# Wider passes in the tail of a streaming encoder step: merges go through DRAM scratch and run beside the last attention blocks, outputs follow tile by tile

## The chip, the cores and the metric

One core of a Trainium2 chip runs the whole program. The metric is the device time of one execution in microseconds (us), median of several runs. The engines are PE (TensorE, matmuls; PEld is its weight load), DVE (VectorE), ACT (ScalarE), POOL (GpSimd) and SP (SyncE, which here issues every DMA). SBUF is the on-chip memory, PSUM the accumulators that PE writes.

## What is computed

One layer of a mixer over 2048 prompt tokens, 16 meta tokens and 8 x 16 sample tokens, width 1024. From the normalised rows h one input projection feeds two branches: gated linear attention (its output, per token, is called `oa` here) and sparse attention over selected keys (`ob`, already gated). Then, per token:

```
y_a    = oa @ w_gla
y_b    = ob @ w_dsa
merged = sigmoid(m_a + gate_b[0]) * y_a + sigmoid(m_b + gate_b[1]) * y_b
h_new  = layer_norm(ALPHA * h + merged @ w_out, ln_g, ln_b)
```

All matrices are 1024 x 1024. The meta tokens need no output, so the tail handles 17 tiles of 128 tokens: prompt tiles 0 to 15 and the sample tile "s". In scratch they stand in the order 0, 1, 2, ..., 15, s.

## The kernel before

Each fp32 product is made of three matmuls: every operand is split into a rounded part `hi` and a remainder `lo` (cast on ACT, subtraction on DVE or POOL), and `mm3` (L265 to L267) adds hi*hi, hi*lo and lo*hi over eight slices of 128 rows, 24 matmuls in all. The weight side of a matmul is 128 x 128, the moving side has as many columns as the piece of tokens is wide.

Phase 1 projects the input and selects keys. Phase 2 runs attention in blocks of 128 queries, 15 down to 8 with the linear attention beside them, and then the tail, which is what the change touches: the blocks of `LAST` (7, 6, 5, 0, 4, 2, 1, 3), and beside and after them three products.

- `gla_project` (L1374) multiplies w_gla with `oa`, 242 tokens a pass in 9 passes (`PASSA`), eight steps of 128 output channels each (24 matmuls, into the one PSUM bank of `pd`), multiplies with the gate `ma` on DVE (`rma`) and stores to the DRAM scratch `d_ya`. It is a generator; `LAST` says how many passes are emitted after each block.
- `merge` (L1392) does the same with w_dsa and `ob`, adds `ya`, and splits the sum into `mh`/`ml`, which stay in SBUF (two pairs of 256 tokens). A step of it is: load `ya` (`rya`) and `mb` (`rmb`), 24 matmuls, multiply and add on DVE, cast on ACT, subtract on POOL.
- `finish` (L1405) merges in chunks of 256 tokens (eight) and one of 128. The first two merges are emitted while attention's pools are still open; then w_out is loaded and split (`woh`, `wol`), and outputs (`fo`, 48 matmuls of 512 columns per 128 tokens, then residual and layer norm) alternate with the next merges.

`w3` (L1339) loads and splits weights. w_gla and w_dsa use the same SBUF tiles `wh`/`wl`, one after the other: each of its eight sets can be reloaded when the last pass of the gated projection has read it. `x3` (L1355) loads and splits four pieces of activations, `rows3` (L1362) loads one 128-row slice into one of two buffers. SP issues the DMAs in the order in which the program has them, and an SP instruction that waits holds up those behind it. The order of all instructions on their engines is laid down at build time by a planner that simulates the program; a block is only given a priority by its place in the code (`early` and `later` shift it). What the lines of a profile call by helper lines: L144 is `tt` (elementwise with two tensors), L153 `stt`, L156 `act`, L159 `copy`, L1347 the cast in `w3`.

## Time and profile before

| | us |
|---|---|
| median of three runs | 3597.57 |
| lowest, highest | 3590.15, 3598.61 |
| profiled execution | 3593.96 |
| its span, first to last instruction | 3592.2 |
| PE busy in it | 3483.6 |
| DVE, ACT, POOL busy | 2528.4, 1450.9, 1088.8 |

The span is what the trace covers; the profiled execution is 1.8 us longer than it. A group of instructions is named by its line, engine, operation and by what it writes and reads (`out<-in`); the shapes are partitions x elements. A matmul's duration in the trace is longer than the distance to the next one, since they overlap. [...]

### The profile page before, as it was taken

Reading aid. Unit: us, or ns where it says so; the run is one execution under the profiler, and the core shown is the slowest. Engines: PE = TensorE matmul, PEld = TensorE weight load, DVE = VectorE, ACT = ScalarE, POOL = GpSimd, SP = SyncE. Lnnn points to the kernel's source line nnn. Section 1 sums busy time; section 2 is a strip of 40 time slices with the busy share of each in tenths; the row PEclk is TensorE's granted clock in tenths of the full one; section 3 lists DMA queues with packets and bytes.
Section 4 is the critical chain, followed back from the end, with each engine's and each line's share of the span. In section 5 each row is a group of like instructions: output and inputs, shape, how many; then the busy total and the mean of one; then the engine's idle time right before and its main releaser. Section 6 shows DMA issues by size and latency. Waiting matters only on the chain. (4 is left out here: it accounts for less than half of the span.)

```text
span 3592.2 us, 66024 instructions
## 1 busy us (share of the span) xinstructions
PE 3483.6 (97%) x24196; PEld 3212.5 (89%) x24196; DVE 2528.4 (70%) x5813; ACT 1450.9 (40%) x3092; POOL 1088.8 (30%) x1412
## 2 busy tenths in 40 slices
PE   7999999999999998999999999999999999989999
PEld 6999999999999998998887788888877888879998
DVE  7737998799999998964436677676765666544444
ACT  4435223433324323322535556566565344331110
POOL 3122242242342334434411345455410000022221
PEclk9999999999999999999999999999999999999999
DMA  8642443254442345445573433333343345564431
GB/s 265 202 131 82 139 121 108 83 157 127 119 145 73 103 134 148 140 134 159 171 199 94 122 109 97 102 105 99 100 121 88 89 120 135 151 192 136 124 115 62
DMA packets 550340, 457.77 MB, mean 127 GB/s; under 512 B 95248, under 2 KB 522528, under 8 KB 550016
## 3 DMA queue, kind: packets, MB, share of 16 engines
q1 hardware_dynamic: 550016, 453.56, 43.9%
q8 instruction: 190, 3.11, 0.4%
q14 instruction: 134, 1.10, 0.1%
HBM read 292.49 MB, written 160.92 MB: 126 GB/s over the span
## 5 line engine op out<-in xcount | busy, mean ns | idle before, releaser
L144 POOL TENSOR_TENSOR wlo<-raw,whi 128x512 fp32r<-128x512 f32 x360 | 482.3, 1360 | 817.1 <-ACT whi L159 706.7
L150 DVE TENSOR_SCALAR_CACHE_REDUCE junk<-sc,cand 128x272 bf16<-128x272 f32 (+6 forms) x512 | 701.6, 1370 | 16.9
L265 PE MATMUL pp<-whi,xh 128*128 128x256 f32 (+3 forms) x1952 | 562.1, 288 | 3.5 <-ACT whi L159 2.3
L265 PE MATMUL pp<-xh,whi 128*128 128x384 f32 (+2 forms) x1728 | 563.6, 326 | 1.9 <-ACT whi L159 1.1
L267 PE MATMUL pp<-whi,xl 128*128 128x256 f32 (+3 forms) x1952 | 560.8, 288 | 4.4 <-DVE xl L144 4.4
L267 PE MATMUL pp<-xh,wlo 128*128 128x384 f32 (+2 forms) x1728 | 563.0, 327 | 1.0 <-POOL wlo L144 1.0
L266 PE MATMUL pp<-xl,whi 128*128 128x384 f32 (+2 forms) x1728 | 563.4, 326 | 0.0
L266 PE MATMUL pp<-wlo,xh 128*128 128x256 f32 (+3 forms) x1952 | 561.9, 288 | 0.0
L265 PEld LDWEIGHTS pp<-whi,xh 128*128 128x128 f32 (+1 forms) x1952 | 371.9, 191 | 12.7 <-issue 4.3
L267 PEld LDWEIGHTS pp<-whi,xl 128*128 128x128 f32 (+1 forms) x1952 | 371.0, 190 | 11.3 <-DVE xl L144 6.9
L266 PEld LDWEIGHTS pp<-wlo,xh 128*128 128x128 f32 (+1 forms) x1952 | 371.5, 190 | 7.8 <-issue 5.2
L1131 DVE CUSTOM_DVE_ANT_0 lgl<-pl,mkl 128x348 f32<-128x348 f32 (+8 forms) x608 | 296.1, 510 | 102.8 <-PE pl L1130 65.8
L265 PE MATMUL pd<-xh,wh 128*128 128x242 f32 (+3 forms) x1152 | 327.7, 285 | 8.2 <-ACT wh L1347 4.5
L159 ACT CAST whi<-raw 128x512 fp32r<-128x512 f32 (+1 forms) x344 | 199.2, 622 | 319.7 <-DMA raw<-in_w_in 204.8
L265 PEld LDWEIGHTS pp<-xh,whi 128*128 128x128 f32 x1728 | 325.1, 188 | 3.3 <-ACT whi L159 1.7
L267 PEld LDWEIGHTS pp<-xh,wlo 128*128 128x128 f32 x1728 | 324.8, 188 | 2.5 <-POOL wlo L144 1.8
L266 PE MATMUL pd<-xl,wh 128*128 128x242 f32 (+3 forms) x1152 | 324.6, 282 | 2.1 <-DVE xl L144 2.1
L266 PEld LDWEIGHTS pp<-xl,whi 128*128 128x128 f32 x1728 | 325.1, 188 | 0.6
L267 PE MATMUL pd<-xh,wl 128*128 128x242 f32 (+3 forms) x1152 | 324.5, 282 | 0.8 <-POOL wl L144 0.8
L156 ACT ACTIVATE lgl<-lgl,mx 128x1040 f32<-128x1040 f32 (+7 forms) x256 | 249.9, 976 | 177.9 <-DVE mx L1133 171.4
L1129 PE MATMUL pl<-kd,q 128*128 128x348 f32 (+14 forms) x800 | 302.5, 381 | 14.1 <-DVE mx L1131 4.9
L1130 PE MATMUL pl<-kd,q 128*128 128x348 f32 (+14 forms) x800 | 261.7, 330 | 0.0
(252 smaller groups left out, 7592.7 us busy)
## 6 DMA issues: line engine op xcount, KB each, us to landing
raw<-in_w_in SPq DMA_DIRECT2D x360, 256.0 KB, 3.2
q<-d_q SPq DMA_DIRECT2D x272, 128.0 KB, 3.0
d_h<-x SPq DMA_DIRECT2D x17, 512.0 KB, 3.3
d_gv<-en SPq DMA_DIRECT2D x68, 128.0 KB, 1.9
d_gr<-en SPq DMA_DIRECT2D x68, 128.0 KB, 2.0
d_z<-en SPq DMA_DIRECT2D x68, 128.0 KB, 1.7
v<-d_gv SPq DMA_DIRECT2D x17, 512.0 KB, 3.7
gr<-d_gr SPq DMA_DIRECT2D x17, 512.0 KB, 3.6
```

The costliest lines, as they stand in the source:

```text
L144: (eng or self.nc.vector).tensor_tensor(out, a, b, op=op)
L150: (eng or self.nc.vector).tensor_scalar(out, a, s1, s2, op0=op0, op1=op1, **kw)
L156: self.nc.scalar.activation(out, a, f, **kw)
L159: (self.nc.vector.tensor_copy if self.spare else self.nc.scalar.copy)(out, src)
L265: mm(ps, ah(k), bh(k), start=k == 0, stop=False)
L266: mm(ps, ah(k), bl(k), start=False, stop=False)
L267: mm(ps, al(k), bh(k), start=False, stop=k == n - 1)
L1129: nc.tensor.matmul(ps[:, :m], q[:, u, :], kd, start=True, stop=False)
L1130: nc.tensor.matmul(ps[:, :m], q[:, 2 + u, :], kd, start=False, stop=True)
L1131: nc.vector.tensor_tensor_reduce(lg[z1][:, a : a + m], ps[:, :m], mk[z1][:, a : a + m], 1.0, NEG, OP.add, OP.max, mx[:, s : s + 1])
```

## The change

`NP3`, the widest piece of tokens, goes from 256 to 384, the raw buffers of `w3` and `x3` (`PRB`) from 2 to 4, and the gated projection is cut into 6 passes of 364 tokens instead of 9 of 242; it now yields after each of its eight steps instead of after a pass. [...]

Merges become a generator of their own, `merges`: five chunks of 384 tokens and one of 256, in an order that begins with tiles 14, 15, s and ends with tiles 0, 1 and then 2, 3, 4. Each step writes `hi` into the `ya` tile and `lo` into the `mb` tile and stores both to DRAM scratch, `d_mh` and `d_ml`. Projection and merges are chained: 8 steps are emitted first, then 72 (`BESIDE`) are spread over the quarters of the last eight blocks in proportion to their numbers of keys, and the 16 steps that are left, tiles 0 and 1 and tiles 2 to 4, are emitted by `finish` after the attention pools are closed and the load of w_out is emitted. Outputs then go by tiles of 128 tokens: each loads its `mh`/`ml` from scratch (the first into a buffer of its own after the ninth of those steps, the others into three buffers in the memory that the merges have left), and then does as before. Half of the weights (four sets) instead of a quarter go to the pool `pw2`, and four sets instead of six are loaded ahead of the first activations.

```
-LAST = [(7, 0), (6, 2), (5, 1), (0, 1), (4, 2), (2, 1), (1, 1), (3, 0)]
-NP3 = 256
+LAST = 7, 6, 5, 0, 4, 2, 1, 3
+DMA_SCRATCH = 1024
+NP3 = 384
-PRB = 2
+PRB = 4
-PASSA = 9
-SHORT = 8
+PASSA = 6
+BESIDE = 72
+MTB = 3
+MERGES = [(14, 3), (11, 3), (8, 3), (5, 3), (0, 2), (2, 3)]
...
-            steps, self.turns = self.gla_project(), TURNS[1]
-            next(steps)
-            for j, n in LAST:
+            steps, self.turns = chain(self.gla_project(), self.merges()), TURNS[1]
+            for _ in range(8):
+                next(steps)
+            total, past, done = sum(nkeys(j) + P for j in LAST), 0, 0
+            for j in LAST:
                 for _ in self.attend(j):
-                    pass
-                for _ in range(n):
-                    next(steps, None)
+                    past += (nkeys(j) + P) / 4
+                    while done * total < BESIDE * past:
+                        next(steps)
+                        done += 1
             self.flush()
-            fin = self.finish()
-            next(fin)
-        next(fin, None)
-        tail.close()
+        self.finish(steps, tail)
...
-            if last and a + 2 * width == DM:
+            if last and a == DM // 2:
                 pool = last
...
-        first = [next(ws) for _ in range(6)]
+        first = [next(ws) for _ in range(4)]
...
+    def merges(self):
+        x, wd = None, None
+        for t, n in MERGES:
+            c0, n = COL[t], n * P
+            x = self.x3("ob", c0, n)
+            wd = wd or list(self.w3(self.pw, self.i["w_dsa"][0], "w", P, last=self.pw2))
+            for q in range(8):
+                ya = self.rows3("ya", c0, n, q)
+                t = self.rows3("mb", c0, n, q)
+                self.tt(t, self.proj3(wd[q], x, n), t, OP.mult)
+                self.tt(t, t, ya, OP.add)
+                hi, lo = ya.bitcast(F32R), t.bitcast(F32R)
+                self.split_sb(hi, lo, t)
+                for name, z in ("mh", hi), ("ml", lo):
+                    self.move(self.d[name][q * P : (q + 1) * P, c0 : c0 + n], z)
+                yield
+
+    def finish(self, merges, before):
...
+            cp, wk, m0, pp = pool("fc"), pool("fk", FKB), pool("fm0"), pool("fo", 4, space=PSUM)
             self.pd = pool("pd2", 2, space=PSUM)
+            wo = list(self.w3(cp, i["w_out"][0], "wo", 512, WOM, wk))
...
+            def merged(pool, t):
+                m = [pool.tile([P, KT, P], F32R, name="m" + x) for x in "hl"]
+                for z, name in zip(m, ("mh", "ml")):
+                    self.move(z[:], d[name][:, COL[t] : COL[t] + P].rearrange("(k p) t -> p k t", p=P))
+                return m
+            for n, _ in enumerate(merges):
+                if n == 8:
+                    m = merged(m0, tiles[0])
+            before.close()
+            m1 = c.enter_context(self.tc.tile_pool(name="fm1", bufs=MTB))
+            for q, t in enumerate(tiles):
+                if q:
+                    m = merged(m1, t)
...
-    nc = bacc.Bacc("TRN2", target_bir_lowering=False, num_devices=1)
+    nc = bacc.Bacc("TRN2", target_bir_lowering=False, num_devices=1, dynamic_dma_scratch_size=DMA_SCRATCH)
```

## Rows read from the trace of the kernel before

**Rows 1.** The page, busy time by engine (us, share of the span, instructions).

```profile
PE 3483.6 (97%) x24196; PEld 3212.5 (89%) x24196; DVE 2528.4 (70%) x5813; ACT 1450.9 (40%) x3092; POOL 1088.8 (30%) x1412
```

**Rows 2.** Stretches of the tail: PE, PEld, DVE, ACT, POOL, clock, DMA.

```profile
core 0: us, PE busy (x) PEld busy (x) DVE busy (x) ACT busy (x) POOL busy (x), PEclk, DMA share, GB/s
2672.00:3100.00 428.00, 417.20 (x3338) 365.23 (x3337) 261.41 (x876) 191.28 (x420) 31.43 (x125) 1.00 0.43 114
...
3170.00:3245.00 75.00, 62.87 (x374) 55.21 (x374) 38.84 (x67) 27.51 (x50) 19.69 (x18) 0.89 0.70 214
3245.00:3500.00 255.00, 255.00 (x1700) 235.93 (x1699) 118.13 (x209) 34.74 (x75) 56.50 (x62) 1.00 0.41 126
```

**Rows 3.** What PE waited for, 3165 to 3245 (us, times, longest).

```profile
PE pd L265 <- ACT wh L1347: 4.5, 2, 2.8
PE oo L1101 <- DVE pm L144: 4.5, 1, 4.5
```

**Rows 4.** The handover's stretch, instructions on `pd` alone (PE, PEld, DVE).

```profile
3170.00:3245.00 75.00, 37.86 (x250) 35.73 (x249) 4.53 (x11) 0.89 0.70 214
```

**Rows 5.** The same stretch, instructions on `fo` alone.

```profile
3170.00:3245.00 75.00, 25.44 (x103) 18.60 (x104) 2.55 (x4) 0.89 0.70 214
```

**Rows 6.** Timeline of PE, first and last of four dense runs (start, duration).

```profile
500.05 0.28 PE L266 MATMUL pp<-wlo,xh 128*128 128x256 f32 x1
501.13 0.28 PE L266 MATMUL pp<-wlo,xh 128*128 128x256 f32 x1
...
999.70 0.33 PE L266 MATMUL pp<-xl,whi 128*128 128x384 f32 x1
1000.91 0.33 PE L267 MATMUL pp<-xh,wlo 128*128 128x384 f32 x1
...
2894.58 0.27 PE L265 MATMUL pd<-xh,wh 128*128 128x242 f32 x1
2896.28 0.28 PE L265 MATMUL pd<-xh,wh 128*128 128x242 f32 x1
...
3547.73 0.28 PE L266 MATMUL pd<-xl,wh 128*128 128x128 f32 x1
3548.96 0.28 PE L265 MATMUL pd<-xh,wh 128*128 128x128 f32 x1
```

**Rows 7.** Groups by line and shape: `pd` at L265, a third each.

```profile
L265 PE MATMUL pd<-xh,wh 128*128 128x256 f32 x512 | 146.9, 288 | 6.8 <-ACT wh L1347 4.5 <-DVE rmb L144 2.3
L265 PE MATMUL pd<-xh,wh 128*128 128x242 f32 x512 | 145.3, 284 | 1.4 <-ACT xh L159 1.2
L265 PE MATMUL pd<-xh,wh 128*128 128x240 f32 x64 | 18.1, 282 | 0.0
L265 PE MATMUL pd<-xh,wh 128*128 128x128 f32 x64 | 17.5, 273 | 0.0
```

**Rows 8.** Groups by shape: the merge's elementwise steps (busy us, mean ns).

```profile
L144 POOL TENSOR_TENSOR mgl<-rmb,mgh 128x256 fp32r<-128x256 f32 x64 | 51.0, 798 | 152.8 <-ACT mgh L159 152.8
L144 DVE TENSOR_TENSOR rmb<-rmb,rya 128x256 f32<-128x256 f32 x64 | 27.5, 429 | 1.8
L144 DVE TENSOR_TENSOR rmb<-pd,rmb 128x256 f32<-128x256 f32 x64 | 26.9, 421 | 87.3 <-PE pd L267 77.7 <-DMA rmb<-d_mb 7.6 <-issue 1.2
L159 ACT CAST mgh<-rmb 128x256 fp32r<-128x256 f32 x64 | 26.0, 406 | 215.5 <-DVE rmb L144 215.5
```

**Rows 9.** DMA issues: issuing engine, count, KB each, median us to landing.

```profile
d_ob<-ob SPq DMA_DIRECT2D x64, 128.0 KB, 2.6
rmb<-d_mb SPq DMA_DIRECT2D x64, 128.0 KB, 2.3
...
iq<-d_ih SPq DMA_DIRECT2D x16, 256.0 KB, 4.5
...
raw<-in_w_out SPq DMA_DIRECT2D x16, 256.0 KB, 4.1
```

**Rows 10.** The chain that ended last, in the handover (start, us, what).

```profile
3184.16 7.08 DMA raw<-in_w_dsa
```

**Rows 11.** Casts of w_out: ns min/median/max, first and last start.

```profile
L1347 ACT CAST woh<-raw x16: 613/618/626, 3183.2 to 3213.5; 128x512 fp32r<-128x512 f32 x16
```

## Prediction

> **What bounds the kernel now.** I read the page's busy shares first: TensorE (PE) is busy for 3483.6 of 3592.2 us [rows 1], so time can only come from fewer or shorter matmuls or from stretches where PE waits. The change touches nothing before the last eight attention blocks, so I next cut the tail, 2672 to 3592 us, into stretches [rows 2]. From 2672 to 3100 PE is busy 417.2 of 428 us, from 3245 to 3500 all of 255. [...]

> A busy PE is not yet a dense one, so the price of a matmul is its distance from the next start, not its duration. From dense runs of the timeline I take the first and the last start and divide [rows 6]: 1.08 us for nine steps at 256 columns, 1.21 for seven at 384, 1.70 for fifteen at 242, 1.23 for eleven at 128, that is 0.120, 0.173, 0.1135 and 0.112 us a matmul. [...]

> **The change, step by step.** The sum is made against the profiled execution, 3593.96 us.

> *Gated projection, 242 to 364 tokens.* Columns stay; passes go from 9 to 6, each of 8 x 24 matmuls. Before: 1536 at 242 and 192 at 240 columns [rows 7], 1728 x 0.1135 = 196.1 us. After: 960 at 364 (0.120 + 108 x 0.00041 = 0.164) and 192 at 356 (0.161) = 188.4 us. Saved: 7.7 us. All of it is PE work in a stretch where PE is the bound, so it counts in full.

> *Merges, eight of 256 and one of 128 tokens, to five of 384 and one of 256.* Before: 1536 x 0.120 + 192 x 0.112 [rows 6, 7] = 184.3 + 21.5 = 205.8 us. After: 960 x 0.173 + 192 x 0.120 = 166.1 + 23.0 = 189.1 us. Saved: 16.7 us, over half of it the 128-token piece, which paid double per column.

> [...]

> *Merges beside the last blocks.* 8 steps run first and 72 are spread by keys, 80 in all: 48 of projection, 32 of merge. Before, 72 shorter ones stood there. The blocks leave PE idle only 10.8 of the 428 us from 2672 to 3100 [rows 2], so the added 32 merge steps cost their full matmul time there and leave the late stretch by the same amount: moved, not saved. What this does buy is the handover. The 75 us from 3170 to 3245 hold 250 x 0.12 + 103 x 0.226 + 21 others at about 0.2 = 57.5 us of dense work; 17.5 us are lost, idle or at the low clock. After, the reload of w_dsa falls under attention matmuls, and when the last block drains PE has the 16 merge steps left over, the first eight (tiles 0, 1) with inputs long stored. I take 17.5 out and leave 2 for the w_dsa reload among the blocks (bounds: 0, and the 4.5 us that PE waits for `wh` now [rows 3]). The idle 11 us among the blocks I leave as they are (bounds: 11 gained with more filler, or 5 lost because a 24-matmul step is now 4.0 us on the one `pd` bank and an attention matmul that is due waits that much longer than the 2.7 us of today).

> *The scratch round trip.* Each merge step now issues four DMAs on SP (load `ya`, load `mb`, store `mh`, store `ml`) instead of two. `hi` and `lo` are written into the loaded tiles, of which there are two each, so a buffer comes back only after: multiply 0.42, add 0.43, cast 0.41, subtract 0.80 [rows 8], store 2.6, reload 2.3 [rows 9], SP issue and semaphores some 0.6: 7.6 us for two steps at 256 tokens, 3.8 a step, where PE needs 2.9. At 384 the engine parts grow by half and the DMAs a little, 3.1 + 5.3 + 0.6 = 9.0, 4.5 a step against 4.15. Beside the blocks the stretch from 2672 to 3170 grows to 498 - 8 + 32 x 4.15 = 623 us, a step every 7.8, so this is hidden; in the last 16 steps nothing else stands before PE, since the outputs wait for w_out: (3.8 - 2.9) x 8 + (4.5 - 4.15) x 8 = 10 us. Those 16 steps also share the queues with w_out: 4 + 6 MB of merge tiles, 2.5 of `ob`, 4 of w_out, 1 of norm rows, 1.5 for the first output tile, 19 MB. At 214 GB/s and a share of 0.70, or 126 at 0.41 [rows 2], a full queue moves about 306 GB/s, so 65 us against 56 us of matmuls; latencies will be those of a loaded queue. I take 13 us lost. Lower bound 0. Upper bound: store and reload 4.1 us each, as w_out's loads now [rows 9]: 5.4 and 5.8 a step, 20 + 13 = 33 us. The one 7.08 us landing in the handover [rows 10] shows that this is no fancy.

> [...]

> *Outputs by tile.* 816 `fo` matmuls at 512 columns before and after, no change. Each tile now loads 1 MB of merged values in rows of 512 B, beside 0.5 MB of `h` and 0.5 MB stored: 2.1 MB in 48 x 0.226 = 10.8 us, 195 GB/s. From 2672 to 3100, where most transfers have rows of 128 or 242 tokens (512 or 968 B), 114 GB/s take a share of 0.43 [rows 2], 265 at full, so 7.9 of 10.8 us: hidden, with three buffers. Costs nothing; if the cover fails, the second rival. The 128-token merge pieces that were interleaved with outputs are gone, and the final drain (last matmul, norm, store) is the same.

> *1 KB for dynamic DMAs* frees room for the wider tiles. The issue rows name SP [rows 9], none of the page names POOL; I put 0.

> Sum: -7.7 - 16.7 - 17.5 + 2 + 13 = -26.9, 3567 us for the profiled frame. The three timed runs before have a median 3.6 above the profiled execution, so I forecast 3569.

> **The rivals.**
> 1. *Everything covered.* The round trip hides behind output tile 14 and the wider steps fill the idle 11 us: -7.7 - 16.7 - 17.5 - 8 = -50, 3545 to 3555, say 3550. For it: PE found filler at once from 3245 on. Against: 19 MB in 56 us. Chance 0.15.
> 2. *Output tiles bound by their loads* (the slower side). Loads of 256 KB in 512 B rows land in 4.5 us [rows 9]; if 1 MB per tile went at that rate, one after another, a tile takes 18 us less overlap, about 14, against 10.8: 17 x 3.2 = 54 us, giving 3569 + 54 = 3623. It decides once a tile's transfers need more than 10.8 us. Against: 7.9 worked out above. Chance 0.10.
> 3. *Loaded round trip*: 33 us instead of 13 in the last 16 steps: 3589. For it: the handover's DMA share of 0.70 [rows 2]. Chance 0.17.
> 4. *The handover stays*: w_out cannot be loaded before attention frees its memory, and if its 16 loads take longer than the 16 merge steps (today its casts spread over 30 us [rows 11], beside w_dsa's), PE stands as before: 3569 + 15.5 = 3585. Chance 0.08.
> [...]

> **How the numbers follow.** The forecast has 0.48, with its own range 3558 to 3582. I call 0.3% (11 us) the least that a measurement of this kernel tells from no change; against the median 3597.57 that is 3587 to 3608. Faster: forecast 0.48, rival 1 0.15, most of rivals 4 and 3 that lie just at the edge 0.12: 0.75. Same: the rest of 3 and 4, and 5: 0.15. Slower: rival 2, 0.10. The range from 3546 to 3598 leaves out rival 2, part of 1 and takes in the 33 us bound.

> **What would show it.** Right: starts of `pd` 0.165 us apart at 364 and 0.173 at 384 columns; PE dense through the last block's end at full clock; gaps of 0.5 to 1.5 us per step in the last 16 merge steps, DVE there waiting for `mb`; outputs at 10.8 us a tile without gaps. Wrong: PE waiting for loads of `mh`/`ml` between tiles (rival 2), a hole before the first `fo` (rival 4), or new waits among the attention blocks, where I expect none.

## The result, and the profile after

The changed kernel takes 3614.17 us (median of 4, 3610.43 to 3616.81) against 3594.98 for the kernel before: a ratio of 1.0055 [1.0039, 1.0071], 20 us slower. I had forecast 3569 with a range to 3598 and put 0.10 on slower, for another reason than the one that the runs found. The profiled execution has a span of 3612.5 us, against 3592.2.

The page of the changed kernel, busy time by engine, answers to [rows 1]:

```profile
PE 3483.2 (96%) x23044; PEld 3194.0 (88%) x23044; DVE 2496.0 (69%) x5717; ACT 1438.6 (40%) x3044; POOL 1084.3 (30%) x1388
```

TensorE runs 1152 fewer matmuls in the same busy time, and the span grew by 20 us. Busy time hides much here: a matmul counts as busy for longer than the distance to the next start (0.33 against 0.167 us below), and where the granted clock was 0.50 of full speed for longer still (0.49 against 0.29 us for a logits matmul of 348 columns at 1888 us). So the first thing to read is again how close together the starts are. The timeline of PE in the changed kernel, first and last of three dense runs (start, duration):

```profile
2999.76 0.33 PE L271 MATMUL pd<-xl,wh 128*128 128x364 f32 x1
3001.93 0.33 PE L272 MATMUL pd<-xh,wl 128*128 128x364 f32 x1
...
3231.38 0.34 PE L270 MATMUL pd<-xh,wh 128*128 128x384 f32 x1
3234.36 0.34 PE L272 MATMUL pd<-xh,wl 128*128 128x384 f32 x1
...
3499.71 0.39 PE L272 MATMUL fo<-woh,ml 128*128 128x512 f32 x1
3503.60 0.39 PE L271 MATMUL fo<-wol,mh 128*128 128x512 f32 x1
```

2.17 us over 13 gaps, 2.98 over 17, 3.89 over 17: 0.167, 0.175 and 0.229 us, where the prediction had 0.164, 0.173 and 0.226. The wider matmuls do nearly what they should; by these starts and the counts of matmuls the two projections take some 20 us less than before (the forecast had 24.4). So some 40 us were lost in other places. The windows of the changed kernel (columns as in [rows 2]) show where:

```profile
1840.00:1960.00 120.00, 106.07 (x612) 86.05 (x612) 64.87 (x215) 51.63 (x109) 17.28 (x33) 0.87 0.54 147
1880.00:1900.00 20.00, 14.73 (x56) 12.15 (x56) 8.40 (x30) 5.34 (x13) 0.65 (x2) 0.54 0.54 125
1960.00:2620.00 660.00, 644.12 (x4416) 533.29 (x4413) 450.45 (x1598) 379.79 (x820) 309.37 (x600) 1.00 0.36 101
...
3338.00:3427.00 89.00, 73.02 (x434) 68.76 (x435) 36.24 (x61) 19.99 (x36) 16.34 (x17) 0.95 0.70 215
3427.00:3604.00 177.00, 177.00 (x766) 144.81 (x766) 85.46 (x122) 0.00 (x0) 22.10 (x15) 0.99 0.58 175
```

Two of the same stretches in the kernel before:

```profile
1840.00:1960.00 120.00, 107.76 (x704) 88.21 (x703) 67.03 (x219) 56.64 (x117) 16.64 (x32) 0.96 0.51 137
1960.00:2620.00 660.00, 650.10 (x4497) 540.91 (x4495) 462.18 (x1644) 391.04 (x839) 311.44 (x604) 1.00 0.38 105
```

In the first 780 us of the second half, whose code the diff does not touch, PE starts 5028 instructions in place of 5201, at a granted clock of 0.87 in place of 0.96 in the first stretch. From 1880 to 1900 the clock is 0.54, in each us up to 1898 it is 0.50, while PE stood again and again before small steps of the sample's attention (PE's waits, 1840 to 1960; us, times, longest):

```profile
PE pg L1229 <- DVE on L148: 4.7, 3, 3.1
PE pg L1209 <- ACT slg L160: 3.6, 2, 2.2
```

If from each start-to-start time the price of its matmul's shape in a dense run is taken away, PE loses some 87 us from 1840 to 2620, where the kernel before loses some 68, 6 to 8 us of the difference before 1960 and about 10 after; all losses below are counted so, and are good to a few us. The handover [rows 2, 3] has not become shorter either: PE is busy 73.0 of 89 us, against 62.9 of 75.

The order of SP's queue is where the first stretch begins to differ. SP at the start of the second half, in the changed kernel (start, duration, what):

```profile
1850.70 0.41 SPq L176 DMA_DIRECT2D kd<-d_kd  x1
...
1858.52 0.46 SPq L1298 DMA_DIRECT2D v<-d_v  x1
1859.07 4.18 SPq L176 DMA_DIRECT2D d_q<-eh  x1
...
1872.40 0.49 SPq L1031 DMA_DIRECT2D mkl<-d_mask  x1
...
1878.93 1.53 SPq L176 DMA_DIRECT2D q<-d_q  x1
```

And in the kernel before:

```profile
1851.70 0.40 SPq L1026 DMA_DIRECT2D mkl<-d_mask  x1
...
1853.20 1.92 SPq L172 DMA_DIRECT2D q<-d_q  x3
...
1859.09 0.89 SPq L172 DMA_DIRECT2D kd<-d_kd  x2
...
1861.23 1.42 SPq L1293 DMA_DIRECT2D v<-d_v  x1
```

Before, the mask and the queries of block 15 go out first, then the keys and the 2 MB of values. After, keys and values come first, mask and queries 21 and 26 us later. The first logits start 20 us later too; here the kernel before, then the changed one:

```profile
1866.89 0.66 PE L1129 MATMUL pl<-kd,q 128*128 128x348 f32 x1 [2.62 <-DMA kd<-d_kd]
...
1887.32 0.64 PE L1134 MATMUL pl<-kd,q 128*128 128x348 f32 x1
```

The second place is the handover. The chain that ended last, there (start, duration, what):

```profile
3347.02 6.13 DMA d_ml<-rmb
...
3354.96 3.87 DMA rmb<-d_mb
...
3360.58 0.41 ACT rya L163
3361.06 0.95 POOL rmb L148
3362.03 4.61 DMA d_ml<-rmb
3366.70 2.80 DMA rmb<-d_mb
...
3371.42 5.26 DMA d_ml<-rmb
```

This is the scratch round trip itself, on the chain that sets the end: store a slice, load the next one into the same buffer, multiply, store. In these rows a store takes 4.6 to 6.1 us and a reload 2.8 to 3.9, where I had 2.6 and 2.3 [rows 9].

### The profile page after: what moved, and what is told of

The parts are those of the page before. It is cut to its first block, busy times and chain, and to the rows that moved or that the text cites. A ratio compares the mean times of both kernels' runs of the same rounds, so it can differ in the third digit from the quotient of the medians.

```text
span 3612.5 us, 63548 instructions
## 1 busy us (share of the span) xinstructions
PE 3483.2 (96%) x23044; PEld 3194.0 (88%) x23044; DVE 2496.0 (69%) x5717; ACT 1438.6 (40%) x3044; POOL 1084.3 (30%) x1388
## 3 DMA queue, kind: packets, MB, share of 16 engines
q8 instruction: 182, 2.98, 0.3%
## 5 line engine op out<-in xcount | busy, mean ns | idle before, releaser
L1136 DVE CUSTOM_DVE_ANT_0 lgl<-pl,mkl 128x348 f32<-128x348 f32 (+8 forms) x608 | 294.9, 510 | 96.1 <-PE pl L1135 65.9
L270 PE MATMUL pd<-xh,wh 128*128 128x364 f32 (+3 forms) x768 | 259.4, 338 | 10.3 <-DVE rmb L148 9.0
L1094 PE MATMUL oo<-pt,v 128*64 128x256 f32 x1088 | 260.5, 388 | 8.1 <-DVE pt L1080 4.3
L1142 POOL COPY pmeta<-lgl 128x48 f32<-128x48 f32 x256 | 61.3, 242 | 663.8 <-ACT lgl L160 662.7
```

What stands on the lines that cost most here:

```text
L270: mm(ps, ah(k), bh(k), start=k == 0, stop=False)
L1094: self.nc.tensor.matmul(oo[0][64 * o : 64 * o + 64, k : k + 2, :], self.v[:, s0 + s, d : d + 64], t[:, 2 * s : 2 * s + 2], start=self.fres ...
L1136: nc.vector.tensor_tensor_reduce(lg[z1][:, a : a + m], ps[:, :m], mk[z1][:, a : a + m], 1.0, NEG, OP.add, OP.max, mx[:, s : s + 1])
```

## The experiments

Theory: (1) the smaller reserve costs nothing itself, but moves the tiles, and so changes the order in which the second half is issued; (2) two slice buffers make the last merge steps wait for their round trip. Rivals: the reserve makes DMAs slower by itself; the handover's loss comes from where the tail happens to start. Each kernel was timed against the kernel before on its own chip, so kernels from different chips are compared by their ratios (0.1% is 3.6 us).

| run | edit | median us | ratio to before |
|---|---|---|---|
| e1_reserve_only | before, small reserve | 3623.57 | 1.0087 [1.0072, 1.0101] |
| e5_reserve_same_places | e1, 15,360 B per partition held | 3593.99 | 1.0004 [0.9993, 1.0015] |
| e2_change_old_places | changed, 15,360 B held until the tail | 3603.15 | 1.0028 [1.0019, 1.0038] |
| e3_four_slices | e2, four slice buffers | 3573.65 | 0.9942 [0.9929, 0.9955] |
| e6_pools_a | changed, other pool order | 3587.7 | 0.9988 [0.9978, 0.9999] |
| e6_pools_b | changed, a third pool order | 3607.47 | 1.0037 [1.0024, 1.0050] |
| e7_four_slices_alone | changed, four slice buffers | 3591.78 | 0.9999 [0.9989, 1.0009] |
| e8_nine_passes | e3, nine passes of 242 | 3596.77 | 1.0009 [0.9999, 1.0019] |
| e9_pools_and_slices | e6_pools_a, four slice buffers | 3565.28 | 0.9932 [0.9916, 0.9948] |
| e10_beside_64 | e9, 64 steps beside the blocks | 3567.57 | 0.9938 [0.9923, 0.9952] |
| e11_reserve_pools_a | e1, pool order of e6_pools_a | 3593.46 | 1.0008 [0.9998, 1.0018] |
| e12_nine_passes_again | e9, nine passes of 242 | 3594.17 | 1.0016 [1.0003, 1.0028] |

**The reserve alone.**

```diff
-    nc = bacc.Bacc("TRN2", target_bir_lowering=False, num_devices=1)
+    nc = bacc.Bacc("TRN2", target_bir_lowering=False, num_devices=1, dynamic_dma_scratch_size=1024)
```

> The kernel before with the reserve for dynamic DMAs set to 1024 bytes and nothing else changed. Theory A (the smaller reserve moves the SBUF pools, the planner lays out another order from the start of phase 2, and that order is slower): 20 to 28 us over the kernel before, 3615 to 3623 us; the stretch from 1840 to about 2640 us of the trace loses as the changed kernel's does. Theory B (the chip serves DMAs worse with the small reserve): the same time, 3615 or more, but then the loss must stand wherever DMAs run, phase 1 included. Theory C (the loss comes from the new tail, which the planner pulls forward): 3595, no change.

Measured: 3623.57 us. The one constant costs the old kernel 31 us, a little over the 20 to 28 that I expected. Its first logits start at 1888.7 us, as in the changed kernel, and its instructions stand in the changed kernel's order up to the tail.

**The reserve with every tile at its old place.** An unused tile of 15,360 bytes per partition stands where the reserve had been.

```diff
+        ctx.enter_context(self.tc.tile_pool(name="spacer", bufs=1)).tile([P, 3840], F32, name="spacer")
```

> The kernel before with the reserve at 1024 bytes and an unused tile of 15360 bytes per partition held throughout, so that every other tile stands where it stood and the order of instructions is that of the kernel before. Theory A: 3595 us, no change within 0.3%. Theory B: 3615 or more.

Measured: 3593.99 us, a ratio of 1.0004 [0.9993, 1.0015], with the order of before on all engines. The reserve by itself costs nothing; that rival falls.

**The change at the old places.** The same tile, given back when the tail begins.

```diff
             early.close()
+            self.spacer.close()
```

> The changed kernel with an unused tile of 15360 bytes per partition held until the tail begins, so that phases 1 and 2 have the places and the order of the kernel before, and the tail is the new one with its room. Theory A: the 20 to 28 us are back, 3586 to 3594 us. Theories B and C: 3614, as the changed kernel. Whatever stands between 3586 and my forecast of 3569 is then owed by the tail.

Measured: 3603.15, only 0.27% (10 us) back. The old order returns up to the tail and with it the old loss before it, but the tail is worse off in this kernel: the first `pd` starts at 2754.8 us, against 2639.6 in the changed kernel, and from 2620 us to the last output PE loses some 5 us more. My expectation of 3586 to 3594 missed. I put that down to the held tile, which takes from the weights of the gated projection the room that it leaves to the rest; no run tests this.

**Four slice buffers there.**

```diff
-            ..., left("pe", 2), left("pw")
+            ..., left("pe", 4), left("pw")
```

> As the run before, with four buffers instead of two for each of the loaded row slices of ya and mb. Theory (the last 16 merge steps are paced by two slice buffers that return only after their store has landed): 8 to 14 us less than the run with two, the waits for mb before the merge's multiplication mostly gone, 3574 to 3584 us. Rival (the DMA queues are full there, 19 MB at some 306 GB/s): within 3 us of the run with two. A second rival: more loads ahead of time in SP's order delay the q loads of the attention blocks, and the gain is given back there.

Measured: 3573.65, 29.5 us below e2 on the same chip, more than twice what I expected. Four buffers are worth more than the prediction's 13 us for the round trip, and this kernel beats the one before. Of the gain, 15 us are lost time after the last block (23 us to 8); the rest lies before it.

**The changed kernel with other pool orders.** No tile held; the same nine pools of the second half are opened in another order on the right-hand side, and nothing else. For e6_pools_a:

```diff
-            self.lg, vp = right("lg", 4), right("v")
-            lower = [None, right("kdl1")]
-            self.az, self.pts, self.sm = right("az"), right("pts", PTB), right("sm", 2)
-            self.st, self.aq = right("st"), right("aq", 2)
-            lower[0] = right("kdl0")
+            lower = [None, None]
+            self.aq = right("aq", 2)
+            self.pts = right("pts", PTB)
+            lower[1] = right("kdl1")
+            self.sm = right("sm", 2)
+            self.az = right("az")
+            self.st = right("st")
+            lower[0] = right("kdl0")
+            vp = right("v")
+            self.lg = right("lg", 4)
```

> The changed kernel with nothing but the order of the right-hand pools of the second half altered, so that on SP's queue the mask and the first queries of block 15 stand ahead of the 2 MB of values and of the second half of the lower keys (in the changed kernel they stand behind both). Theory A, the 18 us lost before the tail come from what the queue puts ahead of the first queries: the first logits start before 1876 us in place of 1887.3, the TensorE time lost between 1840 and 1960 falls from 34.9 to under 30 us, and the median is 3598 to 3606 us. Rival, the loss comes from the order as a whole, not from these loads: within 3 us of the changed kernel's 3614.

Measured: 3587.7, 0.67% (24 us) below the changed kernel, more than the 8 to 16 us that I expected. SP's queue in e6_pools_a:

```profile
1629.51 0.43 SPq L1031 DMA_DIRECT2D mkl<-d_mask  x1
1629.99 0.58 SPq L176 DMA_DIRECT2D q<-d_q  x1
...
1853.89 0.88 SPq L176 DMA_DIRECT2D kd<-d_kd  x2
...
1867.05 0.51 SPq L1303 DMA_DIRECT2D v<-d_v  x1
```

The mask and the first queries now go out 220 us early, in the first half, because their tiles got a place that is free there; the values go last. First logits at 1859.2. The same windows of e6_pools_a:

```profile
1840.00:1960.00 120.00, 105.58 (x692) 85.19 (x691) 68.64 (x230) 59.23 (x121) 16.34 (x33) 0.99 0.49 128
1960.00:2620.00 660.00, 650.96 (x4510) 543.29 (x4510) 458.77 (x1644) 390.90 (x846) 312.08 (x605) 1.00 0.38 104
```

5202 PE instructions in the 780 us, as before the change (5201), the clock is back, and the lost time from 1840 to 2620 is some 69 us, again as before. About 18 of the 24 us thus lie ahead of the tail.

> As the run before, with another order of the same pools: both halves of the lower keys stay ahead of the mask and the queries on SP's queue, the 2 MB of values go behind them. If the values are the larger part of what holds the first queries up: first logits before 1880 us, and 3600 to 3608 us. If the keys are: first logits at 1884 or later and 3610 to 3614. If neither matters: 3611 to 3617.

Measured for e6_pools_b: 3607.47. Its keys go out at 1853.0, the first mask at 1855.1, the values at 1867.3; first logits at 1865.2. So the values behind the queries bring the first logits 22 us forward, as expected, but the time falls only by 0.18% (6.5 us), which the two intervals do not tell from nothing. Its second stretch tells why:

```profile
1840.00:1960.00 120.00, 107.16 (x664) 86.03 (x663) 67.75 (x220) 55.43 (x115) 16.11 (x32) 0.91 0.51 141
1960.00:2620.00 660.00, 645.13 (x4425) 537.71 (x4423) 454.90 (x1613) 381.93 (x828) 310.79 (x602) 0.99 0.37 102
```

From 1960 to 2620 it starts 4425 instructions, like the changed kernel (4416), not like before (4497). It loses some 82 us from 1840 to 2620. The late first queries are thus at most a part of the loss and not the whole: the order that the planner chooses for the blocks that follow differs too. Which of those later swaps costs what was not taken apart.

**Four slice buffers alone.**

> The changed kernel with four buffers for the merge slices in place of two, and nothing else (no placeholder, so the order of the second half is the changed kernel's). If the slices' round trip and the order before the tail are two separate losses: the 29.5 us that four buffers gave between the two kernels with the placeholder come here too, 3582 to 3590 us. If four buffers help only because of where the tail began in those: less than 15 us, 3599 or more.

Measured: 3591.78, 0.56% (20 us) below the changed kernel: between the two cases, near the first. The tail's start is the changed kernel's, so the rival that ties the gain to it falls, though e3's gain was some 10 us larger in that kernel's worse tail. The lost time after the last block falls from 24 us in the changed kernel to 4: the whole gain lies where the last merge steps run.

**Both together.**

> The changed kernel with both single edits together: the pool order of e6_pools_a (3587.7 us) and four slice buffers. If the order at the start of the second half and the slices' round trip are separate losses, the 22.4 us that four buffers gave alone come off 3587.7: 3562 to 3569 us, the fastest of all. If the two repair the same loss: 3580 or more.

Measured: 3565.28, the fastest, 0.56% below e6_pools_a: the same 20 us as alone. The two losses are separate: four buffers are worth the same with either order. 24 us for the order and 20 for the buffers, against the gain of 24 (0.68%) that e9 keeps over the kernel before, make the +20 of the result. PE's waits from the last block on, in the changed kernel (3338 to 3605; us, times, longest):

```profile
PE pd L270 <- DVE rmb L148: 8.0, 3, 4.0
PE fo L270 <- DMA mh<-d_mh: 6.5, 1, 6.5
```

and in e9_pools_and_slices (3302 to 3555):

```profile
PE pd L270 <- DVE rmb L148: 2.2, 2, 1.3
PE fo L270 <- DMA mh<-d_mh: 0.8, 1, 0.8
```

The DVE timeline tells the rate of the late steps. In the changed kernel, 256 columns:

```profile
3356.13 0.42 DVE L148 TENSOR_TENSOR rmb<-pd,rmb 128x256 f32<-128x256 f32 x1 [2.04 <-DMA rmb<-d_mb]
...
3379.61 0.42 DVE L148 TENSOR_TENSOR rmb<-pd,rmb 128x256 f32<-128x256 f32 x1 [3.13 <-DMA rmb<-d_mb]
```

Four steps apart: 5.9 us a step, the multiply idle until its slice is loaded. At 384 columns, six steps apart:

```profile
3388.18 0.56 DVE L148 TENSOR_TENSOR rmb<-pd,rmb 128x384 f32<-128x384 f32 x1 [0.67 <-PE pd L272]
...
3418.68 0.56 DVE L148 TENSOR_TENSOR rmb<-pd,rmb 128x384 f32<-128x384 f32 x1 [4.99 <-DMA rmb<-d_mb]
```

That is 5.1 us a step. In e9_pools_and_slices, 384 columns:

```profile
3351.81 0.56 DVE L148 TENSOR_TENSOR rmb<-pd,rmb 128x384 f32<-128x384 f32 x1 [3.94 <-PE pd L272]
3355.97 0.56 DVE L148 TENSOR_TENSOR rmb<-pd,rmb 128x384 f32<-128x384 f32 x1 [3.01 <-PE pd L272]
```

4.16 us a step, which is the price of 24 matmuls, and the multiply now waits for PE; the steps of 256 columns take 3.8 us there, outputs between them. The 6.5 us for `mh` are a consequence: while the merge steps stood, PE ran all 48 `fo` of the first output tile as filler, so nothing covered the load of the second; in e9 only 33 of the 48 had gone by the last `pd`. The other runs bear this out: where all 48 had gone (both e6, e2, e8, e12) PE then waits 4 to 7 us for `mh`, and where 26 to 33 had (e3, e7, e9, e10) at most 0.8.

**The reserve with that pool order, in the kernel before.**

> The kernel before with the smaller descriptor reserve (3623.6 us) and the pool order of e6_pools_a, nothing else. Its TensorE order is that of e6_pools_a until the tail. If the 30 us of the smaller reserve are the order of the second half that the pools' new places give, this order takes most of them away: 3588 to 3600 us. If the smaller reserve costs the old code something else than that order: 3610 or more.

Measured: 3593.46, 0.78% (28 us) below e1, level with before. Two different remedies, a held tile and another pool order, take the reserve's cost away; the free room has no cost of its own.

**More steps left to the end.**

```diff
-BESIDE = 72
+BESIDE = 64
```

> e9_pools_and_slices with 64 in place of 72 steps spread beside the last blocks, so that 24 merge steps in place of 16 run alone after them (as many as e8_nine_passes had there). If merge steps that run alone are what the scratch round trip is paid in, and the 14 us that e8 lost after its last block beyond the price of its matmuls came from their number: 8 to 15 us above e9. If with four buffers it is all one where a step runs: within 3 us of e9.

Measured: 3567.57, 2 us above e9: no difference. With four buffers it is all one whether a merge step runs beside a block or after it.

**Nine passes again**, in two of the four-slice kernels.

```diff
-PASSA = 6
-BESIDE = 72
+PASSA = 9
+BESIDE = 96
```

> The kernel with old places and four slice buffers (3573.7 us), with the gated projection again in 9 passes of 242 tokens in place of 6 of 364, its steps spread over the same blocks (96 in place of 72 beside them). By the starts in the trace (1728 at 0.1135 us against 1152 at 0.166): 4.9 us more, and with 24 more loads and multiplies 3577 to 3583 us. [...]

> e9_pools_and_slices (3565.3 us) with 9 passes of 242 tokens and 96 steps beside the blocks, the same edit that cost the other four-slice kernel 23 us where the starts of its matmuls account for 7. If the width itself costs 23: 3585 to 3591 us. If the width is worth the 5 to 8 us of its starts and the rest in e8 was this kernel's end (tiles loaded late after the blocks): 3570 to 3576 us.

Measured: 0.67% (24 us) above e3 and 0.84% (30 us) above e9. For e8 I expected 3 to 9; for e12 20 to 26 if the width itself costs that much, 5 to 11 if not. Both came out above, so in these two kernels six passes instead of nine are worth some four to six times what their matmul starts say, which is 5 to 6 us. Most of the rest is lost time: in e12 some 13 us more than in e9 after the last block, where 24 merge steps stand and not 16, and some 10 more in the blocks. The 24 steps alone do not cost that, since e10 has them too. PE's waits from 2640 to 3600 in e12_nine_passes_again:

```profile
PE pl L1134 <- DMA q<-d_q: 9.2, 6, 2.2
PE pd L270 <- DVE rmb L148: 4.7, 4, 2.1
...
PE fo L270 <- DMA mh<-d_mh: 4.1, 1, 4.1
...
PE fo L270 <- ACT woh L1357: 3.5, 2, 3.1
```

and the lines of e9_pools_and_slices that answer to them:

```profile
PE pl L1134 <- DMA q<-d_q: 5.7, 3, 3.4
...
PE pd L270 <- DVE rmb L148: 2.5, 3, 1.3
...
PE fo L270 <- DMA mh<-d_mh: 0.8, 1, 0.8
```

Twenty-four more steps mean 24 more loads and stores of slices on SP's queue, and queries and weights that stand behind them come later; from 2660 to 3280 SP waited 55 times for a `d_ya` store in e12 and 39 times in e9, though in sum only 71.9 against 65.9 us. That this is the cause is argued from these lines, not shown: a kernel with the narrow matmuls but the DMAs of six passes was not made, and what sets most of the 18 to 25 us beyond the starts stays open.

## Why the prediction was wrong

**The step that failed** is the last of the change: "1 KB for dynamic DMAs frees room for the wider tiles ... I put 0". With it fails the premise that the prediction begins with, "The change touches nothing before the last eight attention blocks". I looked only at whether somebody uses the reserve, and found nobody; that half holds (e5: 1.0004). I did not ask what the freed room does to the places of all other tiles, and by that to a planned order. It costs 24 us in the changed kernel (e6_pools_a against it) and 31 in the old one (e1), 16 to 18 of them from 1840 to 2620, in code that the diff does not touch. No rival of mine named it; the slower side stood on output tiles bound by their loads. With that step at its size, my own sum would have been -2.9 and the call "same".

**The scratch round trip** was named with the right mechanism and mis-sized: 13 us, bounds 0 and 33. Two buffers against four measure 20 us [e7, e9] to 30 [e3 against e2]. My 3.8 us a step used medians over the whole kernel [rows 9], of loads and stores that for the most part went out at a DMA share of 0.38 to 0.43; in the handover after the change the share is 0.70, the store on the chain took 4.6 to 6.1 us, and a step of 256 columns 5.9 us, a little over my upper bound of 5.4 (at 384 columns 5.1, under the bound, which by its own terms is 5.95 and not 5.8). Against PE's 2.9 and 4.16 us a step that makes, as an estimate, 8 x 3.0 + 8 x 0.94 = 31 us of gaps, nearly rival 3's 33; PE filled 11 us of them with the first output tile, which leaves the 20 that the runs measure, nearer to the forecast's 13. I also missed what follows: the stalls eat the first output tile as filler, and its absence then exposes the second tile's load for 6.5 us. The 0.6 us for SP's issue and semaphores was my estimate and stands in no row; in the chain above 0.02 us pass from the subtraction to its store, and 0.06 from the store's landing to the reload.

**Gated projection and merges by width.** -7.7 and -16.7: the starts came within 2% of what I took, and some 20 of the 24.4 us of matmul time are gone. The 0.00041 us a column in my sum, and with it the 0.164 us at 364 columns and the 0.226 of an `fo` at 512, were estimates from the 0.120 and 0.173 us at 256 and 384 columns [rows 6], which no run shows; the starts in the changed kernel are 0.167 and 0.229 us apart. The nine-pass runs say that in the two kernels with four buffers the whole worth of the wider gated passes is larger, 24 to 30 us instead of 7.7, in waits that I did not price.

**The handover**, -17.5, came only in part. The low clock in my term was a granted share of 0.50, in the kernel before from some 3176 to 3186 and from 3193 to 3200 us. With four buffers and the good order, PE is busy 73.4 of 78 us from the last block on (e9), and what is lost there and in the outputs is some 9 us against 16 before: 7 us gained where I had 17.5. In the changed kernel, with the round trip in it, it is 24. Together with the matmul starts, and the blocks, whose idle time I left as it was and which wait 5.7 us for queries in e9 and 6.3 in the changed kernel against 4.1 before, this is where the sum without round trip and order is short: -24 measured, -39.9 predicted. With the order at +24, the round trip at 20, the handover at 7 and the starts at 20 my sum would be +19. These sizes come from the runs that it is compared with, so this only says that no large term is missing. (3567 and 3.6 make 3571, not the 3569 of the forecast; the 2 us change nothing.)

**Outputs by tile.** As predicted: 766 matmuls in 177.0 us without a gap after the second tile; 0.231 us each, where I took 0.226. Rival 1 (all covered) is false by the round trip. Rival 2 (3623) is false, though the time came near it. Rival 4 (no w_out in time) is false too: `woh` held PE 0.8 us. The 5 in my 'the rest of 3 and 4, and 5', that a matmul costs only its columns, is false by the starts: 0.112 us at 128 columns, 0.1135 at 242 [rows 6].

That e9, the change with both losses repaired, ends at 3565 us, near the forecast of 3569, is luck: the round trip that I had added is gone there, and the handover that I had taken out is partly still in.

## What to carry to other kernels

In a kernel whose order a planner makes from when places come free, a constant that moves tiles is an edit of everything behind it: give it a term and a rival. Look first at the loads that go out just as a phase begins; they show the new order at once, though here the late first queries were at most a part of its 24 to 31 us. Hold the places still with an unused tile, or reorder pools, to tell such a cost from that of the code. And price a buffer's round trip with the landings of the stretch in which it will run, counting what its stalls use up as filler.

## What was not expected of the hardware

Nothing in the chip's own conduct, but two sizes. Three orders of the same nine pools, with the same instructions, take 3587.7, 3607.5 and 3614.2 us (ratios to the kernel before 0.9988, 1.0037 and 1.0055). And the granted clock was low where PE stood before small steps: between 1880 and 1900 PE is busy 14.7 of 20 us and starts 56 instructions, at a granted clock of 0.54; in the kernel before it is busy 19.4 there and starts 119, at 0.95, in another order.
